# Reordering the steps of eight experts: light experts' steps placed singly between steps of the large ones

## The chip, the core and the metric

The kernel runs on one core of a Trainium2 chip. The metric is the device time in microseconds (us) of one execution. A run was also profiled, and all rows below are of that execution.

## What is computed

Two layers of a decoder trunk. Each has a token mixer (four attention groups), a norm, a channel mixer and an embedding gate. The channel mixer of the second layer is a mixture of experts, and all of the change lies in it:

```python
def swiglu(x, w1, w3, w2):
    return (jax.nn.silu(x @ w1) * (x @ w3)) @ w2

logits = (xf @ w_router)
top_logits, top_e = lax.top_k(logits, TOP_K)          # 2 of 8 experts for each of 256 tokens
gates = jax.nn.softmax(top_logits, axis=-1)
...
out = jnp.zeros((T, D)).at[tok_sorted].add(y[dest] * gate_sorted[:, None])
h = layer_norm(DEEPNORM_ALPHA * h + f, ln_ffn_g[i], ln_ffn_b[i])
```

D is 1024, the inner width 3584, all in float32. Each expert has three matrices of 1024 x 3584 words, that is 42 transfers of 1024 KB; the eight have 336.

## The kernel before

**Ranks and places.** The experts are ranked by their number of tokens (rank 0 is always expert 0). `PLACES` gives ranks 0 to 4 room for 128 tokens, rank 5 for 64, ranks 6 and 7 for 32. The first five are called large here (class `Big`), the last three light (class `Small`). If a rank has more tokens than places, a second pass behind a branch takes the rest; in the profiled run it isn't taken.

**Steps.** The work of an expert is cut along the inner width: four steps for a large one (1024, 1024, 1024 and 512 columns), two for a light one (2048 and 1536). `STEPS` (line 26) lists pairs (rank, step). The loop in `experts_in` (line 1301) does for each pair: the product with w1 (`up`, line 1303), silu on ACT; then the down product with w2 of the *previous* pair (`down`, line 1308); then the product with w3 (line 1311), and on DVE the product of both halves (line 1314). The transposes that make the down product's input (`turn`) are put inside the next pair's w1 product, after half of it (`turn_last`). After an expert's last down product `put_back` scatters the result to the tokens and adds it to `h` (`add_back`, line 1250). `make` gathers the tokens of an expert (one-hot matmuls, transposes) two steps before its first step.

**Large and light differ on the engines.** A large expert's weights are split into a high and a low float32r part: for each 128x1024 unit, ACT writes `whi` (line 102), DVE writes `wlo` (line 110), and TensorE does three matmuls for each 512 columns (lines 136 to 138). A transfer of 1024 KB holds two units, so 12 matmuls of 512 columns. A light expert's weights aren't split: TensorE multiplies the raw words, with the tokens as stationary operand of 32 or 64 columns, four or two such groups side by side (lines 1189 and 1232).

**Queues and buffers.** All weights are loaded on SP's queue, in order, in the order of use, into a ring of twelve buffers of 1024 KB (`raw` 4, `side` 3, `post` 3, `early` 2; `load_raw`, line 78). A load waits until the buffer that it takes has been read: for a large expert by DVE's second split of it, for a light one by TensorE's last matmul of it. Five pairs of split units (`whi`, `wlo`) lie between DVE and TensorE. Rank 0's weights have a fixed address; the others' need the ranks, which SP reads from `ids` (line 1037). A scheduler puts the instructions of each engine in order by the program's order and by what is ready in its own model.

**End of the stage.** `closing` (line 1355) loads and prepares what the gate at the end needs; then the last `put_back`, the branch, a layer norm and the gate follow. The norm takes the row sums of `h` from `sums`, which the last `put_back` leaves as the accumulators of its 512-column adds.

```python
STEPS = [(0, 0), (7, 0), (7, 1), (0, 1), (0, 2), (0, 3)] + [
    (r, c) for r in (1, 2, 6, 3, 4, 5) for c in range(2 if PLACES[r] < 128 else 4)]
...
names = [n for j in range(4) for n, (_, bufs) in rings.items() if j < bufs]
turn[0] += 1
t = chunk(names[turn[0] % len(names)])
```

Of the kernel before, what the change touches and what calls it, by code (L numbers as in the profile page):

```python
# [9 lines left out]
FT = mybir.dt.float32  # L10
# [9 lines left out]
NT = S // 128  # L20
# [2 lines left out]
D_FF, N_EXP = 3584, 8  # L23
NFC = D_FF // 512
PLACES = (128, 128, 128, 128, 128, 64, 32, 32)
STEPS = [(0, 0), (7, 0), (7, 1), (0, 1), (0, 2), (0, 3)] + [
    (r, c) for r in (1, 2, 6, 3, 4, 5) for c in range(2 if PLACES[r] < 128 else 4)]
PLE = 256
ALPHA = (2 * DEPTH) ** 0.25
EPS = 1e-5  # L30
# [22 lines left out]
def body(ctx, tc, nc, I, out):  # L53
# [11 lines left out]
    def work():  # L65
        return ps_tile([128, 512], "wk", 4)
# [289 lines left out]
    def table(name, after=None):  # L356

        if after is None:
            return tc.keep_in_program_order(nc.scalar.preload_act_table_set(name))
        with tc.issue_after(after.ins):  # L360
            return nc.scalar.preload_act_table_set(name)
# [575 lines left out]
    def swiglu_moe(hT, logits, closing):  # L937
        hh, hl = hT
        with tc.tile_pool(name="moe", bufs=1, reuse_waits="tile") as mp:
            hsh = mp.tile([128, NT, D], FR, name="hsh")  # L940
            hsl = mp.tile([128, NT, D], FR, name="hsl")
            sums = pers.tile([128, NT, 2], FT, name="sums", tag="lnsm", bufs=2)
            table("exp_and_others", last["sqrt"])
            lgT = mp.tile([128, D], FT, name="lgT", tag="xs", bufs=1)[:2 * N_EXP, :S]
            for t in range(NT):
# [150 lines left out]
            class Big:  # L1096
# [54 lines left out]
                def put_back(self):  # L1151
                    yh, yl = self.y_split(512, self.y)
                    for f in range(2):
                        fs = slice(f * 512, (f + 1) * 512)
                        for t in range(NT):
                            p = work()
                            nc.tensor.matmul(p, self.ohT[:, t], yh[:, fs], start=True, stop=False)
                            nc.tensor.matmul(p, self.ohT[:, t], yl[:, fs], start=False, stop=True)
                            add_back(t, f, 512, p)

            class Small(Big):
# [75 lines left out]
                def put_back(self):  # L1237
                    w = D // self.q
                    yh, yl = self.y_split(w, [self.y])
                    for f in range(self.q):  # L1240
                        rs = self.rows(f)
                        for t0 in range(0, NT, 512 // w):
                            p = work().rearrange("p (t n) -> p t n", n=w)
                            for t in range(t0, t0 + 512 // w):
                                nc.tensor.matmul(p[:, t - t0], self.ohT[rs, t], yh[rs, :w], start=True, stop=False)
                                nc.tensor.matmul(p[:, t - t0], self.ohT[rs, t], yl[rs, :w], start=False, stop=True)
                            for t in range(t0, t0 + 512 // w):
                                add_back(t, f, w, p[:, t - t0])

            def add_back(t, f, w, p):  # L1250
                fs = slice(f * w, (f + 1) * w)
                nc.vector.scalar_tensor_tensor(h[:, t, fs], h[:, t, fs], 1.0, p, op0=OP.mult, op1=OP.add,
                                               accum_out=sums[:, t, f:f + 1] if w == 512 else None)

            def experts(base):
                with ExitStack() as order:
                    experts_in(base, order)

            def experts_in(base, order):
                places = [128] * N_EXP if base else PLACES  # L1260
                seq = STEPS if base == 0 else [(r, c) for r in range(N_EXP) for c in range(len(Big.cols))]
                first = {}
                for s, (r, c) in enumerate(seq):
                    first.setdefault(r, s)
                halves_ = [0]
                made = {}

                def make(r):
                    n = places[r]
                    got = gather(r, n, PLACES[r] if base else 0, halves_[0])  # L1270
                    if n == 128:
                        halves_[0] ^= 1
                        made[r] = Big(r, got)
                    else:
                        made[r] = Small(r, got, n)

                def make_for(s):
                    for r, f in first.items():
                        if f and max(f - 2, 0) == s and r not in made:
                            make(r)  # L1280

                make(seq[0][0])
                if base == 0:
                    order.enter_context(tc.issue_after(done["oh"].ins))
                    order.enter_context(tc.issue_after(done["hs"].ins))
                if base == 0:
                    for t in range(NT):
                        nc.vector.tensor_scalar(h[:, t], h[:, t], ALPHA, None, op0=OP.mult)
                before_ = g = gT = None

                def turn_last():
                    nonlocal gT
                    if g is not None:
                        gT = before_[0].turn(g, before_[1])

                def finish_last():
                    ex, c = before_
                    if c == len(ex.cols) - 1:
                        ex.put_back()

                for s, (r, c) in enumerate(seq):
                    now = made[r]
                    ps = now.up("moe_w1", c, turn_last)
                    sl = mp.tile([128, 1024], FT, name="sl", tag="sl")
                    for f, p in enumerate(ps):
                        nc.scalar.activation(sl[:, f * 512:f * 512 + p.shape[1]], p, AF.Silu)
                    if before_ is not None:
                        before_[0].down(gT, before_[1])
                    elif len(seq) > 1:
                        make_for(s)  # L1310
                    ps = now.up("moe_w3", c)
                    for f, p in enumerate(ps):
                        fs = slice(f * 512, f * 512 + p.shape[1])
                        nc.vector.scalar_tensor_tensor(sl[:, fs], sl[:, fs], now.gs, p, op0=OP.mult, op1=OP.mult)  # L1314
                    if before_ is not None:
                        make_for(s)
                        finish_last()
                    g, before_ = sl, (now, c)
                turn_last()
                before_[0].down(gT, before_[1])  # L1320
                rest = closing() if base == 0 else None
                finish_last()
                if rest is not None:
                    rest()
# [12 lines left out]
    for i in range(DEPTH):  # L1337
        hT, got = mixer(i, hT, None if i else second)
        with tc.tile_pool(name=f"post{i}", bufs=1, reuse_waits="tile") as pool:
# [7 lines left out]
            else:  # L1347
# [7 lines left out]
                def closing():  # L1355

                    for n in ("early", "post", "side"):
                        del rings[n]
                    n = PLE // 128 * S
                    words = held()  # L1360
                    kept["p"] = [words[:, j * n:(j + 1) * n].rearrange("p (k s) -> p k s", s=S).bitcast(FR)
                                 for j in range(2)]
                    ple_turn(i, pool.tile([128, NT, PLE], FT, name="pt", tag="sg", bufs=1), *kept["p"])
                    kept["proj"] = ple_weights(i, held)
                    raw = load_raw(gate_weights(i, 0)[:, :4], [128, 4, 512])
                    kept["gb"] = load_gb("ffn", i, halves(held()))
                    kept["gate"] = []

                    def split(u):
                        wh, wl = split_unit(raw[:, u:u + 2], held, nc.gpsimd)  # L1370
                        kept["gate"] += [(wh[:, j], wl[:, j]) for j in range(2)]

                    split(0)
                    return lambda: split(2)

                sm = swiglu_moe(hT, got, closing)
            with tc.tile_pool(name=f"gate{i}", bufs=1, reuse_waits="tile") as gp:
                if i % 2:
# [8 lines left out]
                gT = nT  # L1387
# [34 lines left out]
```

## Time and profile before

| | |
|---|---|
| median of 3 runs | 1569.78 us (1566.11 to 1572.61) |
| profiled execution | 1569.5 us, span 1567.7 us |
| busy share of the span: TensorE, DVE, ACT | 94%, 63%, 53% |
| granted TensorE clock, mean | 0.97 |
| read from memory | 454.42 MB, 291 GB/s over the span |

The experts' stage takes the span from about 618 us (first load that needs the ranks) to about 1523 us (last down product); the rest is the first layer, the second mixer, and a tail of some 45 us. In the profile PE is TensorE's matmuls, PEld its weight loads, SPq the sequencer of SyncE, which issues the loads. A matmul's duration overlaps the next one's; the distance of two starts is what one costs in a stream.

### The profile page before, as it was taken

How to read it: one execution, taken by the hardware profiler on the slowest of the kernel's cores; microseconds unless marked ns; L12 is line 12 of the kernel's file. 1: busy time of each engine (PE TensorE's matmuls, PEld its weight loads, DVE VectorE, ACT ScalarE, POOL GpSimd, SP SyncE). 2: the span in 40 equal slices, each digit the busy share in tenths (PEclk: the TensorE clock that was granted, in tenths of full speed). 3: DMA queues.
4: the chain of work that ended last, by engine and by line, in shares of the span. 5: the costliest groups of instructions: out<-in, count | busy, mean ns of one | idle time of the engine just before them, and what ended most of it. 6: DMA issues, size and time to landing. Idle time of an engine off the chain costs nothing. (4 is left out here: it accounts for less than half of the span.)

```text
span 1567.7 us, 19973 instructions
## 1 busy us (share of the span) xinstructions
PE 1467.4 (94%) x7330; PEld 1083.6 (69%) x7330; DVE 991.6 (63%) x1328; ACT 835.4 (53%) x1158; POOL 16.6 (1%) x20
## 2 busy tenths in 40 slices
PE   8999999999999997967899999999878999999988
PEld 6877788888788776613687777876335787775436
DVE  7676654545776758402788888976226888875115
ACT  6656544434555656302676777765125676774014
POOL 1000000000010000000000000000000000000001
PEclk9999999999999998978999999999879999999998
DMA  8553655554254523999999989999999999889993
GB/s 273 178 181 121 222 190 186 181 195 155 93 177 162 202 94 133 421 419 415 411 407 411 342 328 365 343 349 342 421 414 413 410 402 368 341 329 370 380 403 109
DMA packets 125065, 456.84 MB, mean 291 GB/s; under 512 B 10976, under 2 KB 22048, under 8 KB 103200
## 3 DMA queue, kind: packets, MB, share of 16 engines
q1 hardware_dynamic: 124960, 455.50, 76.0%
q8 instruction: 59, 0.97, 0.3%
q14 instruction: 46, 0.38, 0.1%
HBM read 454.42 MB, written 1.05 MB: 291 GB/s over the span
## 5 line engine op out<-in xcount | busy, mean ns | idle before, releaser
L110 DVE TENSOR_TENSOR wlo<-raw,whi 128x1024 fp32r<-128x1024 f32 (+1 forms) x264 | 312.8, 1213 | 96.9 <-ACT whi L102 91.9
L102 ACT ACTIVATE whi<-raw 128x1024 fp32r<-128x1024 f32 (+1 forms) x264 | 269.3, 1051 | 185.0 <-DMA raw<-in_moe_w_dram 74.6
L136 PE MATMUL wk<-whi,xgh 128*128 128x512 f32 x560 | 224.1, 400 | 11.2 <-ACT whi L102 11.1
L137 PE MATMUL wk<-whi,xgl 128*128 128x512 f32 x560 | 222.3, 397 | 0.2 <-DVE xgl L132 0.2
L138 PE MATMUL wk<-wlo,xgh 128*128 128x512 f32 x560 | 201.9, 402 | 3.9 <-DVE wlo L110 3.8
L110 DVE TENSOR_TENSOR wlo<-post,whi 128x1024 fp32r<-128x1024 f32 x136 | 162.5, 1220 | 43.7 <-ACT whi L102 42.1
L110 DVE TENSOR_TENSOR wlo<-side,whi 128x1024 fp32r<-128x1024 f32 x132 | 157.2, 1220 | 14.3 <-ACT whi L102 12.5
L102 ACT ACTIVATE whi<-post 128x1024 fp32r<-128x1024 f32 x136 | 140.0, 1056 | 45.3 <-PE wk L137 31.0
L136 PE MATMUL acc<-whi,gh 128*128 128x512 f32 x392 | 155.4, 396 | 8.5 <-ACT whi L102 7.5
L1314 DVE SCALAR_TENSOR_TENSOR sl<-sl,gs,wk 128x512 f32<-128x512 f32 (+2 forms) x43 | 30.2, 733 | 206.6 <-PE wk L1189 150.7
L137 PE MATMUL acc<-whi,gl 128*128 128x512 f32 x392 | 154.0, 393 | 0.0
L102 ACT ACTIVATE whi<-side 128x1024 fp32r<-128x1024 f32 x132 | 135.5, 1056 | 18.7 <-PE acc L137 10.5
L138 PE MATMUL acc<-wlo,gh 128*128 128x512 f32 x392 | 140.2, 397 | 0.6
L136 PEld LDWEIGHTS wk<-whi,xgh 128*128 128x128 f32 x560 | 107.4, 192 | 37.8 <-ACT whi L102 14.1
L138 PEld LDWEIGHTS wk<-wlo,xgh 128*128 128x128 f32 x560 | 105.4, 192 | 31.5 <-DVE wlo L110 10.0
L137 PEld LDWEIGHTS wk<-whi,xgl 128*128 128x128 f32 x560 | 107.5, 192 | 23.2 <-DVE xgl L132 0.5
L136 PEld LDWEIGHTS acc<-whi,gh 128*128 128x128 f32 x392 | 73.7, 188 | 30.7 <-ACT whi L102 13.2
L136 PE MATMUL wk<-whi,hTh 128*128 128x512 f32 x224 | 88.0, 393 | 0.9 <-ACT whi L102 0.9
L138 PEld LDWEIGHTS acc<-wlo,gh 128*128 128x128 f32 x392 | 72.6, 188 | 22.0 <-DVE wlo L110 6.4
L138 PE MATMUL wk<-wlo,hTh 128*128 128x512 f32 x224 | 87.3, 390 | 0.1
L137 PE MATMUL wk<-whi,hTl 128*128 128x512 f32 x224 | 87.2, 389 | 0.0
L137 PEld LDWEIGHTS acc<-whi,gl 128*128 128x128 f32 x392 | 73.8, 188 | 16.1
(397 smaller groups left out, 2220.9 us busy)
## 6 DMA issues: line engine op xcount, KB each, us to landing
raw<-in_moe_w_dram SPq DMA_DIRECT2D x101, 1024.0 KB, 9.6
side<-in_moe_w_dram SPq DMA_DIRECT2D x73, 1024.0 KB, 10.4
post<-in_moe_w_dram SPq DMA_DIRECT2D x73, 1024.0 KB, 9.0
early<-in_moe_w_dram SPq DMA_DIRECT2D x49, 1024.0 KB, 8.9
raw<-in_w_in_dram SPq DMA_DIRECT2D x20, 1024.0 KB, 6.1
raw<-in_ffn_w_dram SPq DMA_DIRECT2D x19, 1024.0 KB, 5.2
post<-in_ffn_w_dram SPq DMA_DIRECT2D x14, 1024.0 KB, 5.2
raw<-in_moe_w_dram SPq DMA_DIRECT2D x15, 768.0 KB, 15.6
```

What stands on the lines that cost most here:

```text
L102: nc.scalar.activation(hi, v, AF.Copy)
L110: engine.tensor_sub(lo, v, hi.bitcast(FT))
L136: nc.tensor.matmul(ps, xh, wh, start=first, stop=False)
L137: nc.tensor.matmul(ps, xl, wh, start=False, stop=False)
L138: return nc.tensor.matmul(ps, xh, wl, start=False, stop=last)
L1314: nc.vector.scalar_tensor_tensor(sl[:, fs], sl[:, fs], now.gs, p, op0=OP.mult, op1=OP.mult)
```

## The change

`STEPS` becomes a written-out list. Both steps of rank 7 stood together as second and third step, both of rank 6 between ranks 2 and 3, both of rank 5 at the end. Now (7, 0) follows (0, 0) and (7, 1) stands inside rank 1; both of rank 5 stand inside rank 2, (6, 0) inside rank 3, and (6, 1) is the last step. The first step turns and does its down product at once, so the second step has none. Since a 32-place expert is now last, its adds of 256 columns leave accumulators too, in a small new tile `quarters`, from which a DVE add makes `sums`.

```diff
-STEPS = [(0, 0), (7, 0), (7, 1), (0, 1), (0, 2), (0, 3)] + [
-    (r, c) for r in (1, 2, 6, 3, 4, 5) for c in range(2 if PLACES[r] < 128 else 4)]
+STEPS = ((0, 0), (7, 0), (0, 1), (0, 2), (0, 3), (1, 0), (1, 1), (7, 1), (1, 2), (1, 3), (2, 0), (2, 1),
...
+            quarters = mp.tile([128, NT, 4], FT, name="quarters")
...
+                    if w < 512:
+                        nc.vector.tensor_add(sums, quarters[:, :, :2], quarters[:, :, 2:])
...
-                                               accum_out=sums[:, t, f:f + 1] if w == 512 else None)
+                                               accum_out=(sums if w == 512 else quarters)[:, t, f:f + 1])
...
-                    elif len(seq) > 1:
+                    elif s == 0:
                         make_for(s)
...
                     g, before_ = sl, (now, c)
+                    if s == 0 and base == 0:
+                        turn_last()
+                        now.down(gT, c)
+                        g = before_ = None
```

The last two lines of `STEPS` are `(5, 0), (5, 1), (2, 2), (2, 3), (3, 0), (3, 1), (6, 0), (3, 2), (3, 3), (4, 0), (4, 1), (4, 2), (4, 3), (6, 1)`.

**SP's queue at the start of the stage.** Loads with 128x2x1024 take two rows of units of w1 or w3, those with 128x2048 a piece of w2; all of them belong to rank 0, and `ids` is the read of the ranks. Before:

```order
L86 DMA raw_5372<-in_moe_w3_dram 128x2x1024
L86 DMA post_5221<-in_moe_w1_dram 128x2x1024
L86 DMA early_5243<-in_moe_w1_dram 128x2x1024
L86 DMA post_5350<-in_moe_w3_dram 128x2x1024
L1037 TENSOR_LOAD ids_5024
```

After:

```order
L87 DMA raw_5373<-in_moe_w3_dram 128x2x1024
L87 DMA raw_5415<-in_moe_w2_dram 128x2048
L87 DMA side_5437<-in_moe_w2_dram 128x2048
L87 DMA post_5222<-in_moe_w1_dram 128x2x1024
L87 DMA early_5244<-in_moe_w1_dram 128x2x1024
L87 DMA post_5351<-in_moe_w3_dram 128x2x1024
L1039 TENSOR_LOAD ids_5025
```

Two loads of the first step's w2 now stand ahead of the first `post` load and of the reads of `ids`.

**TensorE at the first down product.** `xe` are the tokens of rank 7, `sl` the activations that `turn` transposes, `gh` and `gl` the two halves of its result, `acc` the down product, `wk` w1 and w3 products. Before, the transposes of the first step (line 1128) stand between rank 7's w1 products, and the first step's down product behind these:

```order
L1189 MATMUL wk_5396<-post_5409,xe_5284 32x512 x4
L1189 MATMUL wk_5396<-early_5415,xe_5284 32x512 x4
L1128 MATMUL wk_5425<-ident_69,sl_5265 128x128 x4
L1128 MATMUL wk_5432<-ident_69,sl_5265 128x128 x4
L1189 MATMUL wk_5396<-raw_5421,xe_5284 32x512 x4
L1189 MATMUL wk_5396<-side_5443,xe_5284 32x512 x4
L1189 MATMUL wk_5396<-post_5449,xe_5284 32x512 x4
L1189 MATMUL wk_5396<-early_5455,xe_5284 32x512 x4
L136 MATMUL acc_5463<-whi_5467,gh_5423 128x512
```

After:

```order
L139 MATMUL wk_5306<-wlo_5386,xgh_5020 128x512
L1130 MATMUL wk_5399<-ident_69,sl_5266 128x128 x4
L1130 MATMUL wk_5406<-ident_69,sl_5266 128x128 x4
L1191 MATMUL wk_5503<-raw_5504,xe_5285 32x512
L137 MATMUL acc_5413<-whi_5417,gh_5397 128x512
```

Only one light matmul now stands between the transposes and the down product that needs their result.

**TensorE where rank 7's second step stands now.** Before, its w1 products (32x384) follow the first step's w3 products (32x512) directly:

```order
L1189 MATMUL wk_5553<-post_5590,xe_5284 32x512 x4
L1189 MATMUL wk_5553<-early_5596,xe_5284 32x512 x4
L1189 MATMUL wk_5603<-raw_5604,xe_5284 32x384 x4
L1202 MATMUL wk_5631<-ident_69,sl_5461 128x128 x4
L1189 MATMUL wk_5603<-side_5610,xe_5284 32x384 x4
```

After, they stand between w3 products of rank 1 and the down product of rank 1 that they put off:

```order
L139 MATMUL wk_6862<-wlo_6942,xgh_5020 128x512
L1191 MATMUL wk_6953<-post_6954,xe_5285 32x384 x4
L1191 MATMUL wk_6953<-early_6960,xe_5285 32x384 x4
L1130 MATMUL wk_6982<-ident_69,sl_6768 128x128 x4
L1130 MATMUL wk_6989<-ident_69,sl_6768 128x128 x4
L1191 MATMUL wk_6953<-raw_6966,xe_5285 32x384 x4
L1191 MATMUL wk_6953<-side_6972,xe_5285 32x384 x4
L1191 MATMUL wk_6953<-post_6978,xe_5285 32x384 x4
L1191 MATMUL wk_6953<-raw_7000,xe_5285 32x384 x4
L1191 MATMUL wk_6953<-raw_7006,xe_5285 32x384 x4
L1191 MATMUL wk_6953<-side_7012,xe_5285 32x384 x4
L137 MATMUL acc_6771<-whi_7022,gh_6980 128x512
```

The pair of rank 7 is torn apart, and on both sides of each half stand matmuls that need split weights.

## Rows read from the trace of the kernel before

**Rows 1.** The page: rate of the transfers in 40 slices of the span.
```profile
GB/s 273 178 181 121 222 190 186 181 195 155 93 177 162 202 94 133 421 419 415 411 407 411 342 328 365 343 349 342 421 414 413 410 402 368 341 329 370 380 403 109
```
**Rows 2.** Busy time by stretch: length, engines' busy (instructions), clock, DMA share, GB/s.
```profile
860.00:1086.00 226.00, 223.06 (x992) 179.13 (x992) 191.84 (x194) 160.50 (x182) 0.00 (x0) 1.00 0.91 343
1086.00:1300.00 214.00, 187.74 (x1084) 123.84 (x1083) 118.49 (x130) 102.68 (x118) 0.00 (x0) 0.92 1.02 410
1300.00:1430.00 130.00, 128.34 (x570) 102.68 (x568) 107.74 (x108) 88.83 (x101) 0.00 (x0) 1.00 0.92 343
```
**Rows 3.** SP's queue: what loads waited for, 618 to 1521 us (us, times, longest).
```profile
SPq L86 <- DVE wlo L110: 423.7, 172, 7.3
```
**Rows 4.** Timeline of PE, the same place in ranks 1 and 2: start, length, instruction.
```profile
831.36 0.63 PE L1128 MATMUL wk<-ident,sl 128*128 128x128 f32 x4
...
960.19 0.63 PE L1128 MATMUL wk<-ident,sl 128*128 128x128 f32 x4
```
**Rows 5.** Timeline of PE: light matmuls with weights at hand, 32 and 64 places.
```profile
1088.98 1.04 PE L1189 MATMUL wk<-raw,xe 128*32 128x512 f32 x8
1089.84 1.04 PE L1189 MATMUL wk<-side,xe 128*32 128x512 f32 x8
...
1436.54 1.89 PE L1189 MATMUL wk<-early,xe 128*64 128x512 f32 x8
1438.26 1.89 PE L1189 MATMUL wk<-raw,xe 128*64 128x512 f32 x8
```
**Rows 6.** Timeline of PE: a light down product without a stock [idle before <-releaser].
```profile
1127.17 1.94 PE L1232 MATMUL acc<-side,ge 128*32 128x256 f32 x16 [1.06 <-DMA side<-in_moe_w_dram]
```
**Rows 7.** Busy time by stretch: around each light expert, then a refill.
```profile
640.80:766.80 126.00, 95.19 (x656) 46.64 (x656) 34.04 (x36) 32.16 (x37) 0.00 (x0) 0.85 1.02 416
1086.40:1203.40 117.00, 92.00 (x659) 47.20 (x658) 34.44 (x45) 31.77 (x39) 0.00 (x0) 0.85 1.02 413
1430.20:1522.80 92.60, 86.93 (x420) 33.20 (x419) 12.69 (x20) 9.49 (x15) 0.00 (x0) 1.00 0.99 395
1086.40:1158.90 72.50, 55.58 (x447) 21.05 (x446) 12.47 (x22) 9.78 (x15) 0.00 (x0) 0.86 1.01 413
766.80:860.00 93.20, 91.99 (x411) 74.34 (x411) 80.85 (x88) 66.77 (x75) 0.00 (x0) 1.00 1.02 410
```
**Rows 8.** Timeline of SP's queue at the start of the stage: loads issued.
```profile
561.57 0.46 SPq L86 DMA_DIRECT2D post<-in_moe_w_dram  x1
598.34 0.37 SPq L86 DMA_DIRECT2D early<-in_moe_w_dram  x1
...
618.00 0.37 SPq L86 DMA_DIRECT2D raw<-in_moe_w_dram  x1
```
**Rows 9.** Timeline of PE: from the first light matmul; from a light to a large step.
```profile
640.83 1.06 PE L1189 MATMUL wk<-raw,xe 128*32 128x512 f32 x8
...
1161.06 0.79 PE L136 MATMUL wk<-whi,xgh 128*128 128x512 f32 x1 [2.15 <-ACT whi L102]
1161.65 0.63 PE L137 MATMUL wk<-whi,xgl 128*128 128x512 f32 x1
1162.08 0.63 PE L136 MATMUL wk<-whi,xgh 128*128 128x512 f32 x1
...
1166.72 0.40 PE L136 MATMUL wk<-whi,xgh 128*128 128x512 f32 x1
...
1167.42 0.39 PE L137 MATMUL wk<-whi,xgl 128*128 128x512 f32 x1
```
**Rows 10.** Groups by line and shape: DVE's adds of the scattered results (us, mean ns).
```profile
L1252 DVE SCALAR_TENSOR_TENSOR h<-h,wk 128x512 f32<-128x512 f32 x24 | 16.0, 683 | 6.4 <-PE wk L1158 6.4
...
L1252 DVE SCALAR_TENSOR_TENSOR h<-h,wk 128x256 f32<-128x256 f32 x16 | 5.5, 413 | 0.0
```
**Rows 11.** Timeline: the turn of rank 5, which nothing covers.
```profile
1507.16 1.14 DVE L1314 SCALAR_TENSOR_TENSOR sl<-sl,gs,wk 128x512 f32<-128x512 f32 x2 [35.88 <-PE wk L1189]
...
1509.46 1.94 PE L1232 MATMUL acc<-post,ge 128*64 128x512 f32 x8 [0.50 <-ACT ge L1203]
```

More of the change, by code (lines that the diff above doesn't have):

```diff
@@ L25 @@
 PLACES = (128, 128, 128, 128, 128, 64, 32, 32)
-STEPS = [(0, 0), (7, 0), (7, 1), (0, 1), (0, 2), (0, 3)] + [
-    (r, c) for r in (1, 2, 6, 3, 4, 5) for c in range(2 if PLACES[r] < 128 else 4)]
+STEPS = ((0, 0), (7, 0), (0, 1), (0, 2), (0, 3), (1, 0), (1, 1), (7, 1), (1, 2), (1, 3), (2, 0), (2, 1),
+         (5, 0), (5, 1), (2, 2), (2, 3), (3, 0), (3, 1), (6, 0), (3, 2), (3, 3), (4, 0), (4, 1), (4, 2),
+         (4, 3), (6, 1))
 PLE = 256
```

## The prediction

> **What bounds the kernel now.** I read the page's rate of transfers first, then the stretches, then SP's waits, then single instructions. The page shows two levels in the experts' stage [rows 1]: from slice 17 on, some slices stand at 410 to 420 GB/s and others at 340 to 370. The stretches tell them apart [rows 2]. From 860 to 1086 us TensorE is busy 223.1 of 226 us and the transfers run at 343 GB/s; from 1300 to 1430 it is 128.3 of 130, again at 343. From 1086 to 1300 it is the other way: 410 GB/s, and TensorE idles 26 of 214 us. So the bound changes. In a long run of large experts TensorE sets the pace, all twelve buffers are full, and SP stands still: its loads waited 423.7 us, 172 times, for DVE's second split, which frees a buffer [rows 3]. Around a light expert the transfers set the pace and TensorE waits. Time is lost when the transfers pause, since the light experts need that time later.
>
> The prices, in loads of 1 MiB (the stage has 336):
> - A load takes 2.54 us when the queue is full: 1.0486 MB at the 413 GB/s around rank 6 [rows 7].
> - A large load costs TensorE 3.07 us: the same transposes stand at 831.36 and 960.19 us, one large expert or 42 loads apart [rows 4]; 128.83 / 42. This holds gathering, turns and put_back. Bare, it is 12 matmuls at 0.233 = 2.80 us: the last two starts of [rows 9] are three matmuls and 0.70 us apart.
> - A light load costs TensorE 0.86 us for 32 places and 1.72 for 64 (the distances of two starts), when the data are there [rows 5]. Once they aren't, each product waits for its load, here 1.06 us [rows 6].
>
> So a large load leaves 0.5 us over for the queue to run ahead, and a light one takes more than it gets. The ring of twelve is a **stock**, and how much it is worth shows around rank 6. From the first light matmul to the pace of the large ones again, 117.0 us, the kernel used 52 loads = 54.5 MB, while 117.0 × 0.413 = 48.3 MB arrived [rows 7]. The stock gave 6.2 MB, that is 15.0 us. Up to the end of the light products alone it gave more: 38 loads = 39.8 MB in 72.5 us, in which 29.9 MB arrived; 9.9 MB or 24 us [rows 7]. Part of that is bought back in the next large loads. I take 15, and keep 24 as the other end. The stock fills again at 410 − 342 GB/s (1.0486 / 3.07 = 342): 93.2 us after rank 7 [rows 7] make 6.3 MB. After that the transfers pause: (410 − 343) / 410 of 226 and 130 us are 37 and 21 us [rows 2]. Some 58 us of transfer time lie idle there. The most that an order can win back is a little more: 326 loads after the reads of the ranks, at 618.0 [rows 8], × 2.54 = 828, would end the stage at about 1446 rather than 1522.8.
>
> **The ledger on the kernel before.** The light stretch from 640.8 takes 126.0 us for 54 loads (its stock was small, since the queue had just started: 56.6 MB used, 126.0 × 0.416 = 52.4 arrived, so 4.2 MB or 10 us). Then 104 large loads × 3.07 = 319.3; rank 6 with 52 loads 117.0; 74 large loads × 3.07 = 227.2; rank 5 with 44 loads, 111.8 − 15 = 96.8 (measured 92.6 [rows 7]). From 640.8 this gives 1527.1; the last stretch ends at 1522.8. The ledger is good to 5 us over 880.
>
> **The change, part by part.** *Order of steps.* Before, the stock is drawn three times, once almost empty. After, there are five places: (7,0), (7,1), rank 5, (6,0), (6,1). Between them lie 42, 30, 30 and 50 large loads, 129, 92, 92 and 153 us, against a refill of some 93. An episode below includes the twelve large loads or so that run at the transfers' pace behind the light ones, and for each I subtract 15.
>
> *First step's down product at once.* Its turn is now bare, as the order of TensorE shows: activations, transposes, split, then the product. The bare turn of rank 5 took 1507.16 to 1509.46 = 2.3 us [rows 11]; with the split into halves that only a large step has I take 3.5. Rank 7's first light product moves behind 48 matmuls × 0.233 = 11.2 us of down product. It therefore starts at 640.8 + 3.5 + 11.2 = 655.5 instead of 640.8. In that time, and before it, transfers gain: SP stood from 561.6 to 598.3 behind a buffer and to 618.0 behind the ranks [rows 8], with 8 of the experts' loads out. Now two w2 loads pass ahead of the first `post` load, so 10 are out, in time that lay idle. I count both as a fuller stock for (7,0): 15 us where it was 10.
>
> *The sum.*
> - (7,0), 32 loads: 81.2 − 15 = 66, to 722. Then 42 large loads: 129, to 850.
> - (7,1), 30 loads: 76.2 − 15 = 61, to 912. Then 30 large: 92, to 1004.
> - Rank 5, 54 loads: 137.1 − 15 = 122, to 1126 (TensorE alone would need 42 × 1.72 + 12 × 3.07 = 109, so the transfers still bound it). Then 30 large: 92, to 1218.
> - (6,0), 36 loads: 91.4 − 15 = 76, to 1295. Then 50 large: 153, to 1448.
> - (6,1), the last 20 loads: 50.8 − 15 = 36, to 1484.
>
> Against 1522.8 that is 39 less. From it go about 5. The loads of the second steps are 768 KB in a buffer of 1 MiB, so the stock drawn there is up to a quarter smaller, 3.8 us at most at (7,1) and at (6,1). And there are more borders: TensorE waited 2.15 us on ACT's `whi` at the step from light to large [rows 9]; most of that lies inside an episode which the transfers bound anyway.
>
> *The end.* Eight adds of 413 ns replace four of 683 [rows 10]: 0.6 us more; the new DVE add is smaller than either, the adds of one token tile run beside the next one's product, so I take 0.3. Behind it nothing changes. In SP's queue the reads of the ranks stand behind two more loads, 2 × 0.37 us of issuing [rows 8], in time in which SP waits for the `post` buffer anyway. `put_back` and `make` are the same in number and stand at other places.
>
> Sum: 1569.5 − 39 + 5 ≈ **1536** for the profiled execution; the median of the runs is 0.3 above it.
>
> **The rivals.**
> - *The transfers never pause again.* If each stretch of large loads is short enough, all of the 58 to 77 us come back: about 1502. Speaks for it: 24 instead of 15 us per draw [rows 7]. Against: 42 and 50 large loads in a row still fill the ring. Chance 0.08.
> - *Borders eat half.* Light steps between large ones give twelve borders for seven. If each costs 3 us on the path and the first turn 3.5 more, some 18 us go: about 1549. For it: the 2.15 us wait on ACT, whose splits queue behind the silu [rows 9]; against: those borders lie where TensorE has time. Chance 0.15.
> - *The refill is too short.* If the stock does not return between two light places, because a refill of 93 us does not fit into 92, the two new draws win nothing: about 1567. Chance 0.06.
> - *Slower: the clock.* After the waits around rank 6 the first large matmuls start 0.43 us apart (1161.65, 1162.08), from 1166.72 on 0.233 [rows 9]; the granted clock is 0.85 over that stretch [rows 7], so TensorE is at the lower of its levels (1.2 instead of 2.4 GHz) for a part of it. Before, this happens twice. If each of four episodes keeps the lower level through all its twelve large loads, 12 × 12 matmuls lose 0.2 us each, 28.5 us per episode, over 100 in all: 34 of gain become a loss, about 1635. It decides when the lower level lasts through more than a third of those loads; in the row it lasts 5 us, less than two loads. Chance 0.06.
>
> Beside this last rival stands a rule of the Trainium skill (TensorE: Matmul & The Clock Gate, HAM oscillation — how this bites in real kernels): bursts of matmuls that are shorter than the wait for the next data fall back to the slow clock at every wait, and the cost of coming back is paid at every burst instead of once. It speaks against putting light steps between large ones. The trace agrees that the clock falls at such waits; by that rule the change would cost, by the ledger it wins.
>
> **How the numbers follow.** The ledger without a rival has 0.65 and ends between 1526 and 1545. What a measurement can tell from no change is 0.5%, 7.8 us. Faster by more: the forecast, the first two rivals, 0.88, less a little for a ledger that may be off more than once: 0.86. Within: the third rival and a part of that, 0.07. Slower: 0.07. Draws of 24 us in place of 15 would give 4 × 9 = 36 more; half of that reaches 1518, and 2 of the 5 us taken off reach 1516. Upwards the borders reach 1549, and the ledger's 5 us with some rounding 1556. The range is 1516 to 1556.
>
> **What would show it.** In the changed kernel TensorE's matmuls should start 3.07 us per load in the large stretches as before, and the wait of SP's loads for DVE's second split should fall from 423.7 us by some 100 or more. The rate should be near 410 from 655 to 790 us and in four further stretches, and 343 only in the later part of the 42 and 50 large loads. The last down product should end near 1490. TensorE's waits on transfers at (7,1), (6,0) and (6,1) should be short, a few us each. It is wrong if the light steps wait as long as rank 6 does now with the ring full ahead of them, if the granted clock in large stretches falls below 0.9, or if TensorE's idle time moves to ACT's and DVE's splits at the borders.

## The result, and the profile after

The changed kernel took 1531.32 us (median of 4 runs, 1529.34 to 1534.13), the kernel before, run beside it, 1571.11 (4 runs, 1566.11 to 1572.61): ratio 0.9753, 95% interval 0.9723 to 0.9784. That is 2.5% faster, where 1536 in a range of 1516 to 1556 had been predicted. The profiled execution of the changed kernel took 1534.1 us, its span is 1532.3 (before 1569.5 and 1567.7).

The page of the changed kernel, the rate in 40 slices of 38.3 us, answers to [rows 1]:

```profile
span 1532.3 us, 19991 instructions
...
GB/s 273 173 201 124 205 187 201 183 179 179 98 146 137 248 175 74 364 385 413 405 414 334 403 406 412 379 380 397 416 406 414 418 410 412 407 414 386 299 360 111
```

Before, nearly half of the slices of the stage stood at 328 to 370. Now it is one at 334 and one at 299, with 364 and 360 at the stage's two ends and a few near 380. Between them lie long stretches above 400.

Where the light steps now stand, read from the timeline of TensorE (start, length, instruction): the first matmul of (7,0)'s main part (a first bit of (7,0) already stands at 640.99, ahead of the down product), of (7,1), (5,0), (6,0) and (6,1), and the last down product.

```profile
653.36 0.63 PE L1191 MATMUL wk<-raw,xe 128*32 128x512 f32 x3
...
845.34 0.53 PE L1191 MATMUL wk<-post,xe 128*32 128x384 f32 x4
...
1008.29 0.65 PE L1191 MATMUL wk<-post,xe 128*64 128x512 f32 x2
...
1224.76 0.64 PE L1191 MATMUL wk<-post,xe 128*32 128x512 f32 x4
...
1451.28 0.53 PE L1191 MATMUL wk<-raw,xe 128*32 128x384 f32 x4
...
1483.90 0.64 PE L1234 MATMUL acc<-early,ge 128*32 128x256 f32 x8 [0.66 <-DMA early<-in_moe_w_dram]
```

Set beside the ledger of the prediction, which gave the end of each part:

| from | to | ledger, us | measured, us |
|---|---|---|---|
| first reads of the ranks | (7,0) | at 655.5 | at 653.4 |
| (7,0) | (7,1) | 194.5 | 192.0 |
| (7,1) | (5,0) | 154 | 163.0 |
| (5,0) | (6,0) | 214 | 216.5 |
| (6,0) | (6,1) | 230 | 226.5 |
| (6,1) | end of the last down product | 36 | 33.3 |
| end | | at 1484 | at 1484.5 |

The stage ends 38.3 us earlier (1522.8 to 1484.5). Of the span only 35.4 us are gained: what follows the stage grew from 44.9 to 47.8.

The stretches of the changed kernel (columns as in [rows 2]): the whole stage, the large experts behind (7,0) and their last 40 us, the 40 us ahead of rank 5, the large ones behind it, the 53 us ahead of (6,1), and (6,1) itself.

```profile
618.00:1484.50 866.50, 817.41 (x4217) 580.96 (x4215) 563.86 (x613) 474.82 (x543) 0.00 (x0) 0.97 1.00 397
...
720.00:845.34 125.34, 123.92 (x547) 99.01 (x545) 106.58 (x110) 88.44 (x100) 0.00 (x0) 1.00 1.00 387
798.00:838.00 40.00, 39.60 (x175) 31.90 (x174) 38.03 (x43) 30.68 (x35) 0.00 (x0) 1.00 0.94 344
978.00:1018.00 40.00, 40.00 (x182) 28.33 (x183) 27.31 (x28) 20.86 (x23) 0.00 (x0) 1.00 0.93 354
1104.00:1224.00 120.00, 117.00 (x534) 89.83 (x531) 93.54 (x105) 78.88 (x91) 0.00 (x0) 1.00 1.02 412
1398.00:1451.00 53.00, 52.14 (x226) 41.12 (x224) 43.65 (x41) 35.28 (x39) 0.00 (x0) 1.00 0.88 322
1451.28:1484.54 33.26, 26.70 (x264) 12.99 (x263) 10.49 (x17) 6.45 (x9) 0.00 (x0) 1.00 1.00 399
```

The whole stage of the kernel before, in the same view:

```profile
618.00:1522.80 904.80, 836.24 (x4232) 578.10 (x4231) 562.79 (x606) 473.83 (x544) 0.00 (x0) 0.96 0.97 383
```

The row from 1104 to 1224 shows the rate without pauses, 412 GB/s. At that rate the bytes of the stage before (904.8 x 383 = 346.5 MB) take 841.1 us, so 63.7 us were pauses; after, 866.5 x 397 = 344.0 MB take 835.0, and 31.5 us are pauses. So 32 of the 38 us are pauses that are gone. The other 6 are 2.5 MB that the stage no longer has to load, about the two w2 loads (2.1 MB) that now pass ahead of the ranks.

TensorE's busy time in the stage fell too, from 836.2 to 817.4 us, and the granted clock rose from 0.96 to 0.97. I don't count this as a second cause: in the kernel before the clock is low around the light experts (0.85), where the transfers ran at 413 and 416 GB/s and set the pace [rows 7].

SP's wait for DVE's second split, 618 to 1486 us, answers to [rows 3]. It fell by 62 us:

```profile
SPq L87 <- DVE wlo L111: 361.7, 159, 7.9
```

What TensorE waited for within the stage (us in total, times, longest), in the kernel before:

```profile
PE wk L136 <- ACT whi L102: 11.1, 4, 3.1
PE acc L1232 <- DMA raw<-in_moe_w_dram: 9.3, 9, 1.7
PE acc L136 <- ACT whi L102: 7.5, 10, 1.7
PE wk L1189 <- DMA post<-in_moe_w_dram: 6.3, 7, 1.1
```

and in the changed kernel:

```profile
PE wk L137 <- ACT whi L103: 13.7, 6, 3.1
PE acc L137 <- ACT whi L103: 7.9, 8, 1.7
PE acc L1234 <- DMA post<-in_moe_w_dram: 5.6, 3, 2.7
PE acc L1234 <- DMA raw<-in_moe_w_dram: 4.6, 5, 1.4
```

All waits of TensorE's light matmuls for transfers together, eight rows in each view, fell from 43.3 to 20.3 us. TensorE's waits for ACT's `whi` rose from 18.6 to 21.6.

### The profile page after: what moved, and what is told of

Its sections match the earlier page's. It is cut to its first block, busy times and chain, and to the rows that moved or that the text cites. A ratio compares the mean times of both kernels' runs of the same rounds, so it can differ in the third digit from the quotient of the medians.

```text
span 1532.3 us, 19991 instructions
## 1 busy us (share of the span) xinstructions
PE 1448.7 (95%) x7330; PEld 1087.2 (71%) x7330; DVE 995.0 (65%) x1346; ACT 837.4 (55%) x1158; POOL 16.3 (1%) x20
## 5 line engine op out<-in xcount | busy, mean ns | idle before, releaser
L111 DVE TENSOR_TENSOR wlo<-post,whi 128x1024 fp32r<-128x1024 f32 x132 | 157.8, 1221 | 70.1 <-ACT whi L103 68.4
L103 ACT ACTIVATE whi<-post 128x1024 fp32r<-128x1024 f32 x132 | 135.7, 1056 | 108.3 <-DMA post<-in_moe_w_dram 62.0
L111 DVE TENSOR_TENSOR wlo<-side,whi 128x1024 fp32r<-128x1024 f32 x136 | 162.4, 1220 | 13.7 <-ACT whi L103 11.8
L103 ACT ACTIVATE whi<-side 128x1024 fp32r<-128x1024 f32 x136 | 139.9, 1057 | 22.3 <-PE acc L138 11.3
L139 PE MATMUL acc<-wlo,gh 128*128 128x512 f32 x392 | 143.4, 397 | 0.5
```

What stands on the lines that cost most here:

```text
L103: nc.scalar.activation(hi, v, AF.Copy)
L111: engine.tensor_sub(lo, v, hi.bitcast(FT))
L139: return nc.tensor.matmul(ps, xh, wl, start=False, stop=last)
```

## The experiments

Each kernel was compared with the kernel before on the same chip. I call the theory of the prediction the stock theory: the buffers let the transfers run ahead, and the change draws on that at more places.

**The first down product alone.** The changed kernel with the old order:

```diff
-STEPS = ((0, 0), (7, 0), (0, 1), (0, 2), (0, 3), (1, 0), (1, 1), (7, 1), (1, 2), (1, 3), (2, 0), (2, 1),
...
+STEPS = ((0, 0), (7, 0), (7, 1), (0, 1), (0, 2), (0, 3), (1, 0), (1, 1), (1, 2), (1, 3), (2, 0), (2, 1), (2, 2), (2, 3), (6, 0), (6, 1), (3, 0), (3, 1), (3, 2), (3, 3), (4, 0), (4, 1), (4, 2), (4, 3), (5, 0), (5, 1))
```

> The first step's down product at once, with the old order of steps. Stock theory (the time comes from drawing the twelve buffers' stock at five places instead of three): no draw is added, so the time is that of the kernel before within 5 us, 1566 to 1572; rank 7's first light product starts near 655 instead of 641, its last large-pace point stays near 767. Rival 'start' (the gain comes from the two w2 loads that go ahead of the ranks): at least 15 us faster than before, 1555 or less.

Measured 1571.39 (10 runs; 1568.06 before, 13 runs), ratio 1.0024, interval 1.0014 to 1.0034. By itself this part costs about 4 us. Rank 7's main part starts at 652.4, near the 655 expected. In its profile the stage ends 1.1 us earlier than in the kernel before, but it also began 2.9 us earlier (see the table of stage lengths below), and what follows takes 3 us more; why the latter, I did not settle. The rival "start" is out.

**The order alone.**

```diff
-                    if s == 0 and base == 0:
-                        turn_last()
-                        now.down(gT, c)
-                        g = before_ = None
```

> The new order, but the first down product stands behind rank 7's w1 product again. Stock theory: four or five draws remain, only the first is smaller by some 5 us: 1530 to 1540. Rival 'start': the gain goes, 1555 or more. Rival 'end' (the gain comes from a 32-place step at the end): 1531.

Measured 1534.71, ratio 0.9777 (0.9756 to 0.9799). So the order alone wins nearly all. Whether the early down product adds anything to it isn't shown: the ratios (0.9777 and 0.9753) differ by 3.8 us, but their intervals overlap. The profiles do not settle it either. First rows of this kernel: the first load that needs the ranks, and two stretches at the start of the stage.

```profile
621.37 0.37 SPq L87 DMA_DIRECT2D raw<-in_moe_w_dram  x1
618.00:640.00 22.00, 21.77 (x104) 17.57 (x104) 19.99 (x40) 16.22 (x20) 0.00 (x0) 1.00 0.80 322
640.00:660.00 20.00, 18.27 (x115) 10.46 (x114) 8.45 (x10) 8.40 (x11) 0.00 (x0) 1.00 1.01 421
```

The same of the changed kernel:

```profile
616.10 0.34 SPq L87 DMA_DIRECT2D post<-in_moe_w_dram  x1
618.00:640.00 22.00, 21.84 (x104) 17.42 (x103) 20.09 (x35) 17.29 (x20) 0.00 (x0) 1.00 1.01 422
640.00:660.00 20.00, 20.00 (x122) 11.92 (x124) 7.41 (x8) 4.73 (x6) 0.00 (x0) 1.00 0.88 345
```

From 618 to 640 the changed kernel moves 22 us x 100 GB/s = 2.2 MB more. But the profiled execution of the order alone ran 4.6 us later already ahead of the stage (the same load at 560.52 and at 555.96), and its first load that needs the ranks is issued 5.3 us later. From 640 to 660, during the first down product, it is the changed kernel that moves less. From that first load to the end of the last down product the order alone takes 866.4 us and the changed kernel 868.4. Its stage ends 3.3 us later because it starts later.

**Rank 6 as a pair again**, with a large step at the end:

```diff
-STEPS = ((0, 0), (7, 0), (0, 1), (0, 2), (0, 3), (1, 0), (1, 1), (7, 1), (1, 2), (1, 3), (2, 0), (2, 1),
...
+STEPS = ((0, 0), (7, 0), (0, 1), (0, 2), (0, 3), (1, 0), (1, 1), (7, 1), (1, 2), (1, 3), (2, 0), (2, 1), (5, 0), (5, 1), (2, 2), (2, 3), (3, 0), (3, 1), (6, 0), (6, 1), (3, 2), (3, 3), (4, 0), (4, 1), (4, 2), (4, 3))
```

> The change, but rank 6's second step stands right behind its first; a large step ends the stage. Stock theory: one draw of 15 to 20 us is lost, 1545 to 1553. Rival 'end': nearly the whole gain goes, 1562 or more. Rival 'borders' (every border between light and large costs about 3 us on the path): one light place fewer is 3 to 6 us faster, 1525 to 1529.

Measured 1557.33 (1552.69 to 1558.17), ratio 0.9933 (0.9916 to 0.9949): by the two ratios 28 us of the gain are lost, by the profiles 19 (span 1550.9; the profiled execution is the fastest of the four). The median is 4 us above the most that the stock theory gave, and 5 below the least of the rival "end". "Borders", faster, is out. In the profile the last down product ends at 1505.1, 20.5 us later than in the changed kernel, and what follows it takes 45.8 us, 2 less:

```profile
1504.67 0.39 PE L137 MATMUL acc<-wlo,gh 128*128 128x512 f32 x1
```

The transfers run on at 404 GB/s up to 1440. The last load of the experts is issued at 1462.7, and TensorE then needs 42 us for the large loads that lie in the buffers, while the transfers have little left to do (90 GB/s from 1470 on). In the changed kernel, which ends with a light step, it needs 17 us behind the last one (1467.4 to 1484.5).

```profile
1462.71 0.34 SPq L85 DMA_DIRECT2D early<-in_moe_w_dram  x1
...
1398.00:1440.00 42.00, 41.22 (x184) 32.89 (x183) 36.37 (x40) 27.50 (x31) 0.00 (x0) 1.00 1.00 404
1470.00:1505.10 35.10, 32.70 (x143) 24.93 (x141) 29.76 (x30) 23.30 (x28) 2.17 (x1) 1.00 0.24 90
```

**Rank 7 as a pair again.** The end of the stage stays as in the change.

```diff
-STEPS = ((0, 0), (7, 0), (0, 1), (0, 2), (0, 3), (1, 0), (1, 1), (7, 1), (1, 2), (1, 3), (2, 0), (2, 1),
...
+STEPS = ((0, 0), (7, 0), (7, 1), (0, 1), (0, 2), (0, 3), (1, 0), (1, 1), (1, 2), (1, 3), (2, 0), (2, 1), (5, 0), (5, 1), (2, 2), (2, 3), (3, 0), (3, 1), (6, 0), (3, 2), (3, 3), (4, 0), (4, 1), (4, 2), (4, 3), (6, 1))
```

> The change, but rank 7's second step stands right behind its first. Stock theory: one draw of 13 to 17 us is lost, 1544 to 1550; a stretch of 80 large loads from about 777 us on runs with pauses of the transfers, near 343 GB/s. Rival 'end': 1531, no change. Rival 'borders': 1525 to 1529.

Measured 1551.63, 2 us above the range, ratio 0.9890 (0.9870 to 0.9910). By the two ratios 21 us are lost, by the profiles 17 (span 1549.3, stage to 1500.8). The end of the stage alone is not the reason then; it is one of several places. The stretch ahead of rank 5 shows the pauses that are back:

```profile
860.00:1020.00 160.00, 158.56 (x710) 127.91 (x710) 137.88 (x141) 117.47 (x134) 0.00 (x0) 1.00 0.91 339
```

160 us x (1 - 339 / 412) = 28 us, where the changed kernel has 40 x (1 - 344 / 412) = 6.6 us ahead of (7,1) and 40 x (1 - 354 / 412) = 5.6 us ahead of rank 5. The 16 us between them are the 16.3 by which the stage ends later.

**A smaller stock**, ten buffers in place of twelve, in the kernel before and in the changed one:

```diff
-        names = [n for j in range(4) for n, (_, bufs) in rings.items() if j < bufs]
+        names = [n for j in range(4) for n, (_, bufs) in rings.items() if j < bufs and n != "early"]
```

> The kernel before with ten instead of twelve buffers in the ring of the experts (the two early ones are left to the end of the stage). Stock theory: two buffers are 2 x 2.54 = 5.1 us of stock less at each of three draws: 10 to 16 us slower than before, 1578 to 1585. Rival 'latency' (the buffers only cover the time from issue to landing, ten are enough): no change within 3 us.

> The change with ten buffers. Stock theory: five draws, so 20 to 26 us slower than the change, 1551 to 1557, about 10 us more than the same cut costs the kernel before. Rivals 'borders' and 'end': the cut costs both kernels the same. Rival 'latency': no change within 3 us.

Measured 1577.80, ratio 1.0067 (1.0046 to 1.0087), and 1558.89, ratio 0.9929 (0.9902 to 0.9956). Two buffers cost the kernel before 10 us and the changed one (0.9929 - 0.9753) x 1570 = 28, give or take some 6 by the intervals. The direction is as expected, the size is not quite: the changed kernel came out 2 us above its range, and it loses 18 us more than the kernel before, where about 10 were expected. The two stages:

```profile
618.00:1530.50 912.50, 837.34 (x4227) 577.08 (x4225) 561.35 (x604) 472.77 (x544) 0.00 (x0) 0.96 0.97 380
...
618.00:1513.60 895.60, 829.29 (x4240) 586.53 (x4240) 568.15 (x623) 480.59 (x550) 0.00 (x0) 0.97 0.98 384
```

By the rates the pauses grew from 63.7 to 71 us and from 31.5 to 61. Part of the latter is a later start: from the first load that needs the ranks to the last down product the cost is 9 us (904.9 to 914.0) and 24 us (868.4 to 892.4). At 5.1 us a draw that is two draws and five. Before, ranks 6 and 5 had a full stock and rank 7 hardly any; after, there are five places. That each of the five lost its 5 us is not shown. The same cut would cost both the same if the gain had nothing to do with the buffers, and nothing if ten were enough. This is the clearest mark of the mechanism.

**More of it: six single steps**, further from the start.

```diff
+STEPS = ((0, 0), (0, 1), (0, 2), (6, 0), (0, 3), (1, 0), (1, 1), (1, 2), (6, 1), (1, 3), (2, 0), (2, 1), (5, 0), (2, 2), (5, 1), (2, 3), (3, 0), (3, 1), (3, 2), (7, 0), (3, 3), (4, 0), (4, 1), (4, 2), (4, 3), (7, 1))
...
+                    if s:
+                        make_for(s)
                     if before_ is not None:
-                        make_for(s)
                         finish_last()
```

> All six light steps singly, 3, 4, 3, 1, 4 and 5 large steps apart, with rank 6 first and rank 5 torn apart too (a gather of rank 6 moves behind the second step). Stock theory: another draw, and the transfers pause less before each: 15 to 23 us faster than the change, 1508 to 1516. Rival 'pauses are gone already': within 5 us of 1531. Rival 'borders' (3 us each): 3 to 6 us slower than the change, 1534 to 1537.

Measured 1524.52 (1522.53 to 1526.96), ratio 0.9716 (0.9699 to 0.9733). Faster than the change by 6 to 7 us, by intervals that just overlap, where 15 to 23 were expected; the size is a miss, and the median lies nearer to the rival 'pauses are gone already' than to the stock theory's range. Its stage as a whole, and the stretches ahead of (6,0), (7,0) and (7,1):

```profile
618.00:1477.00 859.00, 818.07 (x4219) 576.18 (x4218) 566.72 (x613) 475.22 (x544) 0.00 (x0) 0.98 1.00 400
678.00:709.00 31.00, 31.00 (x140) 25.53 (x139) 24.28 (x22) 20.78 (x22) 0.00 (x0) 1.00 0.95 356
1218.00:1252.00 34.00, 33.68 (x151) 26.67 (x153) 27.91 (x28) 22.76 (x26) 0.00 (x0) 1.00 0.94 355
1411.00:1444.00 33.00, 32.45 (x143) 25.73 (x141) 25.54 (x25) 19.31 (x21) 0.00 (x0) 1.00 0.88 321
```

859 x (1 - 400 / 412) = 25 us of pauses are left, from 31.5: the stage is 7.5 us shorter, and 6.5 of it are pauses. Some 16 of them stand in the last three rows, ahead of three of the places that have three to five large steps before them. One of the places, (5,1), stands where nothing paused. From this came the next question.

**Does a place count, or the pause ahead of it?** The change, with rank 5 torn apart by one large step:

```diff
-STEPS = ((0, 0), (7, 0), (0, 1), (0, 2), (0, 3), (1, 0), (1, 1), (7, 1), (1, 2), (1, 3), (2, 0), (2, 1),
...
+STEPS = ((0, 0), (7, 0), (0, 1), (0, 2), (0, 3), (1, 0), (1, 1), (7, 1), (1, 2), (1, 3), (2, 0), (2, 1), (5, 0), (2, 2), (5, 1), (2, 3), (3, 0), (3, 1), (6, 0), (3, 2), (3, 3), (4, 0), (4, 1), (4, 2), (4, 3), (6, 1))
```

> The change with rank 5 torn apart by one large step, (5,0), (2,2), (5,1); nothing else moved. Theory 'count' (every further light place draws some 15 us, as the prediction's sum has it): 15 us faster than the change, near 1516. Theory 'pauses' (an order wins the time that it takes out of the transfers' pauses, and a place with no pause ahead of it wins nothing): in the change the rate stands above 400 GB/s all the way from 1104 to 1225, so nothing is there to win, 1528 to 1534.

Measured 1531.94 (1530.82 to 1532.80), ratio 0.9759 (0.9731 to 0.9787), the same as the change. So this further place won nothing, and there was no pause behind rank 5 for it to take away (412 GB/s from 1104 to 1224 in the changed kernel). Its stage has the same rate as that of the changed kernel, and the same sum of pauses, 864.3 x (1 - 397 / 412) = 31.5 us:

```profile
618.00:1482.30 864.30, 819.28 (x4214) 577.96 (x4212) 563.24 (x611) 473.34 (x543) 0.00 (x0) 0.97 1.00 397
```

**The length of the stage in each.** What stands ahead of the stage took up to 6.5 us more or less from one profiled execution to the next. So the end of a stage alone can mislead by some us. Its length, from the first load that needs the ranks to the end of the last down product, is the better measure (with the early down product, two of the w2 loads stand ahead of that first load):

| kernel | first load, us | end, us | length, us |
|---|---|---|---|
| before | 618.00 | 1522.86 | 904.9 |
| first down product alone | 615.13 | 1521.71 | 906.6 |
| changed | 616.10 | 1484.54 | 868.4 |
| order alone | 621.37 | 1487.80 | 866.4 |
| rank 6 as a pair | 614.86 | 1505.06 | 890.2 |
| rank 7 as a pair | 616.43 | 1500.78 | 884.4 |
| before, ten buffers | 616.49 | 1530.52 | 914.0 |
| changed, ten buffers | 621.18 | 1513.56 | 892.4 |
| six single steps | 616.61 | 1477.03 | 860.4 |
| rank 5 apart | 615.37 | 1482.30 | 866.9 |

Each line is one execution; differences of 2 us (the first down product in either order, rank 5 apart) I don't take as shown.

**The add of the quarters.** In the changed kernel this add of 128x4 words takes 2.02 us in the tail, beside POOL's splitting (timeline of DVE and POOL):

```profile
1491.00 2.35 POOL L111 TENSOR_TENSOR side<-raw,side 128x1024 fp32r<-128x1024 f32 x1 [1034.13 <-DVE post L111]
1491.34 2.02 DVE L1252 TENSOR_TENSOR sums<-quarters 128x4 f32<-128x4 f32 x1
```

Two kernels ask why, by another form of the add and by POOL left idle:

```diff
-                        nc.vector.tensor_add(sums, quarters[:, :, :2], quarters[:, :, 2:])
+                        nc.vector.scalar_tensor_tensor(sums, quarters[:, :, :2], 1.0, quarters[:, :, 2:],
+                                                       op0=OP.mult, op1=OP.add)
```

> The change, where the sum of the quarters is written as a scalar-tensor-tensor operation instead of a plain add. In the change that add of 128x4 took 2.02 us while POOL was splitting. Theory 'form' (the plain add waits while POOL works, the other form doesn't): 0.1 to 0.3 us and the stage behind it about 1.8 us earlier. Rival 'accumulators' (it waits for the accumulators' writes): 2.0 again.

```diff
-                        wh, wl = split_unit(raw[:, u:u + 2], held, nc.gpsimd)
+                        wh, wl = split_unit(raw[:, u:u + 2], held, nc.vector)
```

> The change, where the two units that are split ahead of the gate are split on DVE instead of POOL. Theory 'POOL' (the add of the quarters takes 2.0 us because POOL works beside it; the same add took 0.16 us behind rank 7, where POOL is idle): 0.2 us for the add. Rival 'accumulators': 2.0 again. The two splits cost DVE 2 x 1.2 us, so the whole stays within 3 us of 1531.

The other form took 1.84 us (1535.12 us, one run):

```profile
1491.05 2.86 POOL L111 TENSOR_TENSOR side<-raw,side 128x1024 fp32r<-128x1024 f32 x1 [1032.37 <-SPq L1338]
1492.08 1.84 DVE L1252 SCALAR_TENSOR_TENSOR sums<-quarters 128x4 f32<-128x4 f32 x1
```

With the split on DVE the plain add took 0.16 us, and the splits 2.36 us behind it:

```profile
1493.95 0.16 DVE L1252 TENSOR_TENSOR sums<-quarters 128x4 f32<-128x4 f32 x1
1494.06 2.36 DVE L111 TENSOR_TENSOR side<-raw,side 128x1024 fp32r<-128x1024 f32 x2
```

It is POOL, and neither the form nor the accumulators. In both slow cases the add ends when POOL's first instruction does (1491.00 + 2.35 = 1493.35 and 1491.34 + 2.02 = 1493.36; 1493.91 and 1493.92). The Trainium skill (GPSIMD Engine Reference, Specifications) has it that VectorE and GpSimd share their interfaces to SBUF, and that VectorE's instructions with two inputs from SBUF contend; the trace agrees. As a whole the kernel with the splits on DVE took 1534.15 (0.9775, interval 0.9742 to 0.9809), no faster than the change: DVE does the splits itself behind the add, and the norm's first instruction starts 10.5 us behind the last down product, where it was 10.6.

**The candidate for the fastest**: the spread order, and the splits on DVE.

> The spread order with the split on DVE: the candidate for the fastest. 1521 to 1526, 5 to 10 us faster than the change.

Measured 1527.16 (1522.49 to 1531.27), 1 us above the range, ratio 0.9738 (0.9707 to 0.9770), no different from the spread order alone. The spread order remains the best that I found, 2.8% faster than the kernel before.

## Why the prediction was right, point by point

**The bound changes along the stage: right.** Long stretches of large experts ran with TensorE busy and the transfers paused, and the changed kernel removes half of the pauses, 63.7 to 31.5 us. The cut to ten buffers, which costs the changed kernel 24 to 28 us and the kernel before 9 to 10, shows that the stock carries it.

**The ledger: right as a sum, with errors that cancel.** The stage ends at 1484.5, where the parts gave 1484 and the forecast, with 5 us taken off, 1490. The part from (7,1) to rank 5 took 9 us more than the 154 of the ledger, the others up to 4 less. The ledger let the transfers set the pace behind (7,1), less a draw of 15 us. There TensorE waited for transfers 0.9 us in all. It was busy for 155.6 of 163.0 us, at a granted clock of 0.95, so it was TensorE that set most of the pace:

```profile
845.34:1008.29 162.95, 155.64 (x828) 117.98 (x828) 116.95 (x136) 98.44 (x112) 0.00 (x0) 0.95 1.01 402
```

The 5 us that were taken off for smaller loads and borders did not appear in the stage; they are not far from the 3 us that the tail cost instead. The 39 us also set the ledger's end after (1484) against the measured end before (1522.8); the ledger's own end before was 1527.1, and ledger against ledger gives 43. So the nearness of 1536 to the 1534.1 of the profiled execution is in part luck.

**"I take 15" for each draw: about right for the two places that were undone, wrong as a rule.** Pairing rank 7 again made the stage 16 us longer, pairing rank 6 again 22. But a further place without a pause ahead of it brought nothing (rank 5 apart), and six single steps brought 6 to 7 us of the 15 to 23. The step that fails is the reckoning by the number of places; what counts is the pause ahead of each. The prediction had the right number beside it, the 58 us that lie idle, and took it only as an upper limit.

**"SP's wait should fall by some 100 or more": wrong.** It fell by 62. The pauses fell by 32 us only; SP also waits for a buffer while earlier loads are still under way, so its wait is larger than the pause and is no measure of it. From 1104 to 1224, where the transfers ran at 412 GB/s, it waited 55.9 us for DVE's second split.

**TensorE's waits on transfers, "a few us each": right.** They are 0.9 us at (7,1), 6.9 at (6,0) and 3.6 at (6,1), where rank 6 had 14.8 before.

**Where the pauses would be left: half right.** They stand in the last part of the 42 and of the 50 large loads (344 and 322 GB/s), as said, but also ahead of rank 5 (354), where the ledger saw a stock that only just fills.

**The first down product: right in time, its worth not shown.** Rank 7's main part starts at 653.4, predicted 655.5. The prediction counted a fuller stock for (7,0), 15 us in place of 10. No run shows this gain: with the old order the early down product costs 4 us, and with the new one the ratios differ by 3.8 us the other way, with overlapping intervals and a stage that is no shorter.

**The end: mis-sized.** I put 0.3 us on the adds. The tail grew by 2.9 us: 2.4 up to the norm's first instruction (8.2 to 10.6 us behind the last down product), in which the small add takes 2.02 us instead of the 0.16 without POOL, and 0.5 behind it. But these 1.9 us are not a net loss. The kernel before lost 1.4 us beside POOL too, at the norm's first instruction with two inputs from SBUF, 2.69 us, where the next of the same kind, behind POOL's, takes 1.28, as both do in the changed kernel (POOL's two splits stand from 1528.11 to 1532.98):

```profile
1531.37 2.69 DVE L379 SCALAR_TENSOR_TENSOR raw<-h,lnnm,post 128x1024 f32<-128x1024 f32 x1
```

What else lengthened the tail stays open; with the first down product alone it grew by 3 us without any such add.

**The rivals.** That the transfers never pause again did not come: 31.5 us of pauses are left. The refill was long enough, since the transfers paused again ahead of rank 5 (354 GB/s). The borders show as 3 us more of waits for ACT's `whi` in the whole stage, not 3 at each new one. The clock does fall, and it does so in the first large matmuls behind (7,0) as it did behind rank 6 [rows 9]:

```profile
653.36:720.00 66.64, 54.48 (x372) 32.41 (x372) 23.39 (x22) 22.30 (x26) 0.00 (x0) 0.87 0.99 399
```

```profile
702.27 0.79 PE L137 MATMUL wk<-whi,xgh 128*128 128x512 f32 x1 [2.21 <-ACT whi L103]
702.86 0.63 PE L138 MATMUL wk<-whi,xgl 128*128 128x512 f32 x1
...
710.75 0.39 PE L137 MATMUL wk<-whi,xgh 128*128 128x512 f32 x1
710.98 0.39 PE L138 MATMUL wk<-whi,xgl 128*128 128x512 f32 x1
```

The granted clock is 0.87 there. The first start after the wait is 0.59 us ahead of the next, and 8 us later starts are 0.23 apart again. Counted over the stage, large matmuls that start 0.40 to 0.46 us apart are 35 before and 57 after; at 0.2 us each that is some 4 us more (a rough count, since a few of them stand singly, far from any wait), not over 100. The lower level lasts a small part of each episode, as the row before had it, and over the whole stage the granted clock is 0.97, before 0.96. The rule of the Trainium skill that the prediction weighed (TensorE: Matmul & The Clock Gate, HAM oscillation — how this bites in real kernels) says that with bursts shorter than the waits the clock falls at every wait, and that the return is paid at every burst. The trace agrees that the clock falls; the cost that this adds here, by the count above, is a tenth of what is won.

## What to carry to other kernels

Where some phases are bound by transfers and others by an engine, look for the time in which the transfers stand still, and place the transfer-bound work just ahead of the point where the buffers fill. In these runs the time won was about the pause that was taken out, and its limit is the sum of the pauses, so read the rate by stretch before counting places. Compare stages by their length, from the same load on, and not by their end. A test with two buffers fewer, in both kernels, tells whether the buffers carry the gain.

## What the runs showed that I had not expected

An add of 128x4 words on DVE took 2.02 us beside a POOL instruction and 0.16 us without, and it ended to the hundredth when POOL's instruction ended. The kernel before had such a place as well, unnoticed. And two buffers of twelve cost the faster kernel two and a half to three times as much (24 us of stage, 28 by the ratios) as the slower one (9 and 10): of these two orders, the better one depends more on the stock.
